# Split float32 products with the high parts first, one low-part buffer, ten row buffers and six 512-column tiles

## The chip, the cores and the metric

The kernel runs on one core of a Trainium2 chip. The metric is the device time of one execution in microseconds: 4555.81 us is the median of three executions before the change (4544.87 to 4565.71). TensorE multiplies into PSUM, VectorE and ScalarE do the elementwise work, GpSimd issues the gathers by index, and SyncE (SP) issues the other transfers. Each engine runs its own queue in order, and an instruction that waits for a semaphore holds back all that stand behind it on that engine.

## The reference, cut to what matters

One step of a hybrid decoder layer on a prompt of 1024 tokens of width 1024 and on eight sample tokens. Three mixers (an SSD state scan, a convolution of width 31, attention over a memory of 256 tokens) are fed from one projection; a gated sum of them goes through an output projection and a norm; then come the experts, and a second norm.

```
proj = x @ w_in
...
x = _layer_norm(ALPHA * x + merged @ w_out, ln1_g, ln1_b)
x = _layer_norm(ALPHA * x + _peer_ffn(x, ...), ln2_g, ln2_b)
```

The experts (PEER) choose, for each token and each of eight heads, 16 of 128 x 128 experts. Each chosen expert is one row of `peer_u` (a dot product with the token, then gelu, then the gate) and one row of `peer_v` (added with that weight):

```
qv = (t @ w_q).reshape(nt, PEER_HEADS, 2, PEER_DHALF)
s = jnp.einsum('thkd,hknd->thkn', qv, sub_keys)
...
act = jax.nn.gelu(jnp.einsum('td,thkd->thk', t, u), approximate=False)
return jnp.einsum('thk,thkd->td', gate * act, v)
```

## The kernel before

The prompt is worked off in three groups of 256, 384 and 384 tokens, features on the partitions. Per group `front` projects and starts the scan, `main` does the mixers and the output projection, `norm1` and `routing` norm and choose the experts.

**Products.** `product` multiplies one 1024 x 128 piece of a weight with the group's tokens, eight matmuls over the contraction. For the input projection and for the experts' first table the operands are split into a high part, rounded to float32r, and a low part, the rest: `load_w` loads `wr` (four buffers), ScalarE copies it to `wh` (L189), VectorE subtracts to `wl` (L191), and `mm3` runs three matmuls for each of the eight pieces of the contraction: high by high, high by low, low by high (L200). The other products run plain float32 from `wr` (L211).

**Gathered experts, groups 0 and 1.** While the next group is in `main`, `spread`, called before every product, sets some row steps of the group before into the queues, by a table of paces; each counts as a late instruction of low priority. `block_u` gathers one row of `peer_u` for each of 128 tokens into a buffer `uv` (GpSimd L442, 512 KB), and VectorE multiplies it with the tokens and sums (L455). `block_v` gathers four rows of `peer_v`, and TensorE adds them up by 32-column strips into `va` (L501). Near the end `block_v2` does that sum on VectorE instead (L544). All these rows share the buffers `uv`, eight of 4 KB a partition (`UVB`).

**Group 2: all experts, densely.** `dense_group` goes through 128 blocks c of 128 experts. `activations` makes the gelu of a product of `peer_ut` with all tokens; `weigh` multiplies with the gates (L1353); `split` makes the high and low part of the result (L176, `b` from `acc`). Then the block of `peer_v` is loaded in two halves into 512-column tiles `e` (`E2B`, seven), split into `vh` and `vl` (L164, L176), and 18 matmuls add into six PSUM tiles (L1385, three token blocks by two halves by three pairs of parts). The first 24 products after the first six are made earlier and read back from `ad`. `wh`/`vh` share a name with two buffers, and so do `wl`/`vl`. The rest of group 1's rows ride along here. The last norm takes its scale and shift rows through buffers of `wl`.

**What sets the order.** The program is scheduled before it runs: instructions are ordered per engine by priority and by when their inputs and buffers are free in the scheduler's own model, and the tiles get their places in that order. So a change of a buffer count can move any instruction. `blk` tiles are 28 general blocks of 392 columns.

Of the kernel before, what the change touches and what calls it, by code (L numbers as in the profile page):

```python
# [9 lines left out]
F32R = mybir.dt.float32r  # L10
# [8 lines left out]
P = 128  # L19
# [5 lines left out]
TB = N // P  # L25
# [4 lines left out]
EPS = 1e-5  # L30
NEG = -3.0e38
TAPS = 31
UVB = 8
TICKS = (4, 6, 5)
PTICK = (1, 1, 0)

# [10 lines left out]
STEP = 4  # L47
VLAG = 6
TLAG = 10
E2B = 7  # L50
BLKB = 28
WRB = 4

C_CW, C_CB, C_D, C_NW = 0, 96, 120, 136
# [9 lines left out]
def f32(ap):  # L64
    return ap.bitcast(F32)
# [3 lines left out]
def hybrid_layer(ctx: ExitStack, tc, I, O):  # L69
    nc = tc.nc  # L70
    pe, act, dve, pool, sp = nc.tensor, nc.scalar, nc.vector, nc.gpsimd, nc.sync
# [3 lines left out]
    accp = ctx.enter_context(tc.tile_pool(name="accp", bufs=8))  # L75
    blkp = ctx.enter_context(tc.tile_pool(name="blkp", bufs=BLKB))
    rawp = ctx.enter_context(tc.tile_pool(name="rawp", bufs=3))
    wp = ctx.enter_context(tc.tile_pool(name="wp", bufs=3))
# [11 lines left out]
    def e2(dt=F32):  # L90
        return ep.tile([P, 512], dt, name="e2", bufs=E2B)

# [88 lines left out]
    def load_raw(src):  # L181
        wr = wp.tile([P, 8, P], F32, name="wr", bufs=WRB)
        sp.dma_start(wr, src)
        return wr

    def load_w(src):
        wr = load_raw(src)
        wh = wp.tile([P, 8, P], F32R, name="wh", bufs=2)
        act.activation(wh, wr, AF.Copy)  # L189
        wl = wp.tile([P, 8, P], F32R, name="wl", bufs=2)  # L190
        dve.tensor_tensor(wl, wr, f32(wh), op=OP.subtract)  # L191
        return wh, wl

    def mm3(ps, w, xh, xl, nk=8, k0=0):
        wh, wl = w
        n = 3 * nk
        i = 0
        for k in range(nk):
            for a, b in ((wh, xh), (wh, xl), (wl, xh)):
                pe.matmul(ps, a[:, k], b[k0 + k], start=(i == 0), stop=(i == n - 1))  # L200
                i += 1

    def product(ps, src, xs):

# [220 lines left out]
    def layer_norm2(r, pn, junk, rows=None):  # L425

        s = rp.tile([P, 4], F32, name="ln2d" if rows else "ln2s", bufs=2)[:pn]
        dve.tensor_reduce(s[:, 0:1], r, axis=AX.X, op=OP.add)
        act.activation(s[:, 1:2], s[:, 0:1], AF.Copy, scale=-1.0 / D)
        act.activation(junk, r, AF.Square, bias=s[:, 1:2], accum_out=s[:, 2:3])  # L430
        act.activation(s[:, 3:4], s[:, 2:3], AF.Ln, scale=1.0 / D, bias=eps[:pn])
        act.activation(s[:, 3:4], s[:, 3:4], AF.Exp, scale=-0.5)
        rpool, rname, rbufs = rows or (pep, "uv", UVB)
        g2 = rpool.tile([P, D], F32, name=rname, bufs=rbufs)
        sp.dma_start(g2, I["ln2"][0:1].to_broadcast([P, D]))
        dve.scalar_tensor_tensor(r, r, s[:, 1:2], g2[:pn], op0=OP.add, op1=OP.mult)
        b2 = rpool.tile([P, D], F32, name=rname, bufs=rbufs)
        sp.dma_start(b2, I["ln2"][1:2].to_broadcast([P, D]))
        dve.scalar_tensor_tensor(r, r, s[:, 3:4], b2[:pn], op0=OP.mult, op1=OP.add)

    def gather(dst, table, idx_col):
        pool.indirect_dma_start(out=dst, out_offset=None, in_=table,  # L442
                                in_offset=bass.IndirectOffsetOnAxis(ap=idx_col, axis=0))
# [3 lines left out]
    def block_u(g, c, idx, gate):  # L447
# [4 lines left out]
        for s in range(P):  # L452
            u = pep.tile([P, D], F32, name="uv", bufs=UVB)
            gather(u, I["peer_u"], idx[:, c, s:s + 1])
# [25 lines left out]
    def block_v(g, c, idx, av, avt, ixt):  # L480
# [23 lines left out]
        for m in range(32):  # L504
            vs = []
            for j in range(4):
                v = pep.tile([P, D], F32, name="uv", bufs=UVB)
                gather(v, I["peer_v"], ixt[:, 32 * j + m:32 * j + m + 1])
# [7 lines left out]
        while not done:  # L516
            yield
        xr = pep.tile([P, D], F32, name="uv", bufs=UVB)
        sp.dma_start(xr, x1d[g][c])
# [3 lines left out]
        active.pop()  # L523
        layer_norm2(xr, P, pep.tile([P, D], F32, name="uv", bufs=UVB))
        sp.dma_start(O[f"yp{g}"][c], xr)

    def block_v2(g, c, idx, av):

        acc = pep.tile([P, D], F32, name="uv", bufs=UVB)
        yield from second_table(P, P, idx[:, c], av, acc)  # L530
# [6 lines left out]
    def second_table(pn, ns, idx, av, acc):  # L537
        for s in range(ns):
            v = pep.tile([P, D], F32, name="uv", bufs=UVB)[:pn]
            gather(v, I["peer_v"], idx[:, s:s + 1])  # L540
            if s == 0:
                dve.tensor_scalar(acc, v, av[:, 0:1], None, op0=OP.mult)
            else:
                dve.scalar_tensor_tensor(acc, v, av[:, s:s + 1], acc, op0=OP.mult, op1=OP.add)  # L544
            yield
# [739 lines left out]
    def dense_group(G):  # L1285
# [50 lines left out]
        while active:  # L1336
            due[:] = 0.0, 8.0
            spread()
        outs = [psp.tile([P, 512], F32, name=nm, bufs=nb)
                for nm, nb in (("mm", 2), ("mm", 2), ("ss", 2), ("ss", 2), ("va", 2), ("va", 2))]  # L1340
# [18 lines left out]
        for c in range(P):  # L1359
            if c + PRE < P:  # L1360
                if c == 2 * EARLY:
                    keep_tokens(G)
                pace[0] = PACE[-2 if c + PRE < early else -1]
                if c + PRE < early:
                    spread()
                    a = accp.tile([P, NW], F32, name="acc")[:, :nt]
                    sp.dma_start(a, ad[:, c + PRE])
                else:
                    a = activations(c + PRE, xs)
                ahead.append(a)  # L1370
                weigh(c + PRE)
            if c + 1 < P:
                ahead[c + 1] = split(ahead[c + 1], nt)
            vh, vl = (wp.tile([P, 1024], F32R, name=n, bufs=2) for n in ("wh", "wl"))
            for dh in range(2):
                hs = slice(dh * 512, dh * 512 + 512)
                v = e2()
                sp.dma_start(v, I["peer_v"][c * P:(c + 1) * P, hs])
                split(v, 512, hl=(vh[:, hs], vl[:, hs]))
            (ah, al), ahead[c] = ahead[c], None  # L1380
            for tbk in range(TB):
                ts = slice(tbk * P, (tbk + 1) * P)
                for i, (a, v) in enumerate(((ah, vh), (ah, vl), (al, vh))):
                    for dh in range(2):
                        pe.matmul(outs[2 * tbk + dh], a[:, ts], v[:, dh * 512:dh * 512 + 512],  # L1385
                                  start=(c == 0 and i == 0), stop=(c == P - 1 and i == 2))
        for tbk in range(TB):
            x1 = wp.tile([P, D], F32, name="wr", bufs=WRB)
            sp.dma_start(x1, x1d[g][tbk])
            for dh in range(2):  # L1390
                hs = slice(dh * 512, dh * 512 + 512)
                dve.scalar_tensor_tensor(x1[:, hs], x1[:, hs], ALPHA, outs[2 * tbk + dh], op0=OP.mult, op1=OP.add)
            junk = wp.tile([P, D], F32, name="wh", bufs=2)
            layer_norm2(x1, P, junk, (wp, "wl", 2))
            sp.dma_start(O[f"yp{g}"][tbk], x1)

    bg.append(memory())
# [120 lines left out]
```

## Time and profile before

| | |
|---|---|
| median of 3 executions | 4555.81 us (4544.87, 4555.81, 4565.71) |
| the profiled execution | 4556.38 us, span 4554.6 us |
| TensorE matmul busy | 3933.1 us (86%), 19901 matmul records |
| weight loads | 3047.6 us (67%), beside the matmuls |
| VectorE | 3289.7 us (72%) |
| ScalarE | 1751.8 us (38%) |
| GpSimd | 1593.4 us (35%) |
| moved by DMA | 1199.42 MB, mean 263 GB/s |
| mean granted TensorE clock | 0.936 |

"Span" is the time from the first to the last instruction of the profiled execution, and all rows are of that execution. "Busy" is time in which an engine works; a wait is the idle time of an engine in front of an instruction, put down to what ended it. Matmuls overlap each other: a product's length is read from the chain of waits, where each piece lasts until the next begins, rather than from the duration of its matmuls. Where the text says 1000 to 1400 us, it is counted from the start of the span: group 0 takes up to about 850, group 1 to about 1950, group 2's mixers to about 2950, then routing and the start of the dense stage to about 3560.

### The profile page before, as it was taken

To read this page: it belongs to the slowest core of one execution; us is meant where nothing else is said; L and a number is where in the kernel's file an instruction comes from. 1 tells how busy PE (TensorE), PEld (TensorE's weight loads), DVE (VectorE), ACT (ScalarE), POOL (GpSimd) and SP (SyncE) were. 2 spreads that over 40 slices of the span, in tenths; PEclk is the share of its full clock that TensorE was granted. 3 is DMA by queue.
4 is the path that set the end of the run, shared out by engine and by line. 5 is a ranking of instruction groups with operands and counts; after the bars stand their busy time and mean duration, and the time that the engine had idled before them with its cause. 6 is when DMAs were issued, how large, how long until landed. Compare 5 with 4: busy or idle time off the path is not lost. (4 is left out here: it accounts for less than half of the span.)

```text
span 4554.6 us, 58299 instructions
## 1 busy us (share of the span) xinstructions
PE 3933.1 (86%) x19901; PEld 3047.6 (67%) x19901; DVE 3289.7 (72%) x7235; ACT 1751.8 (38%) x3696; POOL 1593.4 (35%) x1316
## 2 busy tenths in 40 slices
PE   8998899688898788975888888888996999889996
PEld 8888788567675455553665665445664788778895
DVE  4458835869698546675766796458996899888876
ACT  5475525346432204342362332113562333333333
POOL 0000000123333554413444536534322566556631
PEclk9999999899899998987999999999997999999998
DMA  5435555556677898835878879978879999999985
GB/s 176 149 124 171 180 164 169 202 205 226 220 241 245 302 343 311 291 139 178 282 282 321 304 260 337 341 236 282 305 283 312 359 382 393 343 317 304 389 280 188
DMA packets 410043, 1199.42 MB, mean 263 GB/s; under 512 B 42465, under 2 KB 111713, under 8 KB 407569
## 3 DMA queue, kind: packets, MB, share of 16 engines
q0 software_dynamic: 186880, 679.56, 42.2%
q1 hardware_dynamic: 222864, 516.13, 32.8%
q8 instruction: 157, 2.57, 0.2%
q14 instruction: 142, 1.16, 0.1%
HBM read 1141.59 MB, written 53.93 MB: 262 GB/s over the span
## 5 line engine op out<-in xcount | busy, mean ns | idle before, releaser
L442 POOL DMA_INDIRECT uv<-in_peer_u,idx x640 | 759.0, 1186 | 1831.9 <-DVE idx L422 852.1
L200 PE MATMUL mm<-xt,wh 128*128 128x384 f32 (+1 forms) x4224 | 1045.5, 333 | 37.5 <-ACT b L923 23.9
L455 DVE SCALAR_TENSOR_TENSOR uv<-uv,x 128x1024 f32<-128x1024 f32 x640 | 775.7, 1220 | 395.0 <-DMA uv<-in_peer_u,idx 347.1
L200 PEld LDWEIGHTS mm<-xt,wh 128*128 128x128 f32 x4224 | 745.3, 193 | 100.3 <-issue 33.1
L211 PE MATMUL mm<-b,wr 128*128 128x256 f32 (+2 forms) x2304 | 724.9, 467 | 60.9 <-ACT b L739 34.1
L200 PE MATMUL mm<-xt,wl 128*128 128x384 f32 (+1 forms) x2112 | 692.0, 328 | 37.7 <-DVE wl L191 37.5
L189 ACT ACTIVATE wh<-wr 128x1024 fp32r<-128x1024 f32 x362 | 382.9, 1058 | 864.4 <-PE mm L200 327.0
L442 POOL DMA_INDIRECT uv<-in_peer_v,ixt x384 | 427.6, 1113 | 688.1 <-PE va L501 205.5
L211 PEld LDWEIGHTS mm<-b,wr 128*128 128x128 f32 x2304 | 438.4, 196 | 310.3 <-issue 45.4
L191 DVE TENSOR_TENSOR wl<-wr,wh 128x1024 fp32r<-128x1024 f32 x362 | 441.9, 1221 | 247.1 <-ACT wh L189 229.6
L442 POOL DMA_INDIRECT uv<-in_peer_v,idx x256 | 348.2, 1360 | 345.0 <-DVE uv L544 194.2
L200 PEld LDWEIGHTS mm<-xt,wl 128*128 128x128 f32 x2112 | 406.9, 193 | 57.6 <-DVE wl L191 43.4
L678 DVE SCALAR_TENSOR_TENSOR b<-raw,cc,b 128x384 f32<-128x384 f32 (+1 forms) x720 | 408.7, 569 | 9.9 <-ACT b L676 3.4
L544 DVE SCALAR_TENSOR_TENSOR uv<-uv,av 128x1024 f32<-128x1024 f32 (+1 forms) x269 | 343.5, 1280 | 12.9 <-DMA uv<-in_peer_v,idx 9.9
L501 PE MATMUL va<-uv,slide 128*32 128x512 f32 x1536 | 228.2, 714 | 133.3 <-DMA uv<-in_peer_v,ixt 133.3
L501 PEld LDWEIGHTS va<-uv,slide 128*32 128x32 f32 x1536 | 45.0, 120 | 244.4 <-DMA uv<-in_peer_v,ixt 148.6
L200 PE MATMUL st<-b,wh 128*128 128x384 f32 x784 | 205.7, 344 | 0.5 <-ACT b L832 0.5
L200 PE MATMUL tp<-b,wh 128*128 128x384 f32 x784 | 204.5, 342 | 0.0
L164 ACT ACTIVATE b<-acc 128x384 fp32r<-128x384 f32 x128 | 66.8, 525 | 348.4 <-PE va L1385 261.7
L176 DVE TENSOR_TENSOR wl<-e,wh 128x512 fp32r<-128x512 f32 x256 | 165.1, 684 | 24.2 <-ACT wh L164 22.1
L1385 PE MATMUL mm<-wh,b 128*128 128x512 f32 x512 | 165.2, 404 | 13.7 <-ACT b L164 10.1
L1385 PE MATMUL va<-wh,b 128*128 128x512 f32 x512 | 164.5, 403 | 10.9 <-DVE uv L522 10.9
(409 smaller groups left out, 6382.8 us busy)
## 6 DMA issues: line engine op xcount, KB each, us to landing
wr<-in_win SPq DMA_DIRECT2D x264, 512.0 KB
wr<-in_peer_ut SPq DMA_DIRECT2D x128, 512.0 KB
e<-in_peer_v SPq DMA_DIRECT2D x256, 256.0 KB
wr<-in_wso SPq DMA_DIRECT2D x48, 512.0 KB
wr<-in_wq SPq DMA_DIRECT2D x48, 512.0 KB
gd<-xt SPq DMA_DIRECT2D x16, 1536.0 KB
xt<-gd SPq DMA_DIRECT2D x16, 1536.0 KB
wr<-in_wmo SPq DMA_DIRECT2D x24, 512.0 KB
```

What stands on the lines that cost most here:

```text
L164: act.activation(hi, src, AF.Copy)
L176: dve.tensor_tensor(l, src, f32(h), op=OP.subtract)
L189: act.activation(wh, wr, AF.Copy)
L191: dve.tensor_tensor(wl, wr, f32(wh), op=OP.subtract)
L200: pe.matmul(ps, a[:, k], b[k0 + k], start=(i == 0), stop=(i == n - 1))
L211: pe.matmul(ps, w[:, k], xs[k], start=(k == 0), stop=(k == 7))
L442: pool.indirect_dma_start(out=dst, out_offset=None, in_=table, in_offset=bass.IndirectOffsetOnAxis(ap=idx_col, axis=0))
L455: dve.scalar_tensor_tensor(u, u, 1.0, x1, op0=OP.mult, op1=OP.mult, accum_out=av[:, s:s + 1])
L501: before = pe.matmul(va[dh][32 * j:32 * j + 32], w[:, j, 31 - m:63 - m], vs[j][:, dh * 512:dh * 512 + 512], start=(m == 0), stop=(m == 31) ...
L544: dve.scalar_tensor_tensor(acc, v, av[:, s:s + 1], acc, op0=OP.mult, op1=OP.add)
L678: dve.scalar_tensor_tensor(cv, raw[:, i:i + nt], col(C_FW, j * TAPS + i), cv, op0=OP.mult, op1=OP.add)
L1385: pe.matmul(outs[2 * tbk + dh], a[:, ts], v[:, dh * 512:dh * 512 + 512], start=(c == 0 and i == 0), stop=(c == P - 1 and i == 2))
```

## The change

The matmuls of a split product are the same, in another order: first, for each piece of the contraction, the two that read the high part of the weight, then all that read the low part. For the experts' values the three token blocks first run high by high and low by high, then all run high by low. `wl` and `vl` have one buffer instead of two. `UVB` goes from eight to ten, `E2B` from seven to six, `BLKB` from 28 to 27, and the scale and shift rows of the last norm take buffers of `wr`.

```diff
-UVB = 8
+UVB = 10
...
-E2B = 7
-BLKB = 28
+E2B = 6
+BLKB = 27
...
-        wl = wp.tile([P, 8, P], F32R, name="wl", bufs=2)
+        wl = wp.tile([P, 8, P], F32R, name="wl", bufs=1)
...
-        for k in range(nk):
-            for a, b in ((wh, xh), (wh, xl), (wl, xh)):
-                pe.matmul(ps, a[:, k], b[k0 + k], start=(i == 0), stop=(i == n - 1))
-                i += 1
+        for k, a, b in [(k, wh, x) for k in range(nk) for x in (xh, xl)] + [(k, wl, xh) for k in range(nk)]:
+            pe.matmul(ps, a[:, k], b[k0 + k], start=(i == 0), stop=(i == n - 1))
+            i += 1
...
-            vh, vl = (wp.tile([P, 1024], F32R, name=n, bufs=2) for n in ("wh", "wl"))
+            vh, vl = (wp.tile([P, 1024], F32R, name=n, bufs=nb) for n, nb in (("wh", 2), ("wl", 1)))
...
-            for tbk in range(TB):
+            for tbk, i, a, v in ([(t, i, a, vh) for t in range(TB) for i, a in enumerate((ah, al))]
+                                 + [(t, 2, ah, vl) for t in range(TB)]):
                 ts = slice(tbk * P, (tbk + 1) * P)
-                for i, (a, v) in enumerate(((ah, vh), (ah, vl), (al, vh))):
-                    for dh in range(2):
-                        pe.matmul(outs[2 * tbk + dh], a[:, ts], v[:, dh * 512:dh * 512 + 512],
-                                  start=(c == 0 and i == 0), stop=(c == P - 1 and i == 2))
+                for dh in range(2):
+                    pe.matmul(outs[2 * tbk + dh], a[:, ts], v[:, dh * 512:dh * 512 + 512],
+                              start=(c == 0 and i == 0), stop=(c == P - 1 and i == 2))
...
-            layer_norm2(x1, P, junk, (wp, "wl", 2))
+            layer_norm2(x1, P, junk, (wp, "wr", WRB))
```

The order of the built programs shows what moves. On TensorE in the dense stage, before: the end of a block's activation product (into PSUM tile `tp`, weights `wh`/`wl`) and the first matmuls of the expert values (into `mm` and `ss`, where `wh`/`wl` are the value parts):

```order
L200 MATMUL tp<-b,wh 128x384 x2
L200 MATMUL tp<-b,wl 128x384
L1385 MATMUL mm<-wh,b 128x512 x2
L1385 MATMUL mm<-wl,b 128x512 x2
L1385 MATMUL mm<-wh,b 128x512 x2
L1385 MATMUL ss<-wh,b 128x512 x2
L1385 MATMUL ss<-wl,b 128x512 x2
```

The same block on TensorE after the change, whole:

```order
L199 MATMUL tp<-b,wh 128x384 x16
L199 MATMUL tp<-b,wl 128x384 x8
L1384 MATMUL mm<-wh,b 128x512 x4
L1384 MATMUL ss<-wh,b 128x512 x4
L1384 MATMUL va<-wh,b 128x512 x4
L1384 MATMUL mm<-wl,b 128x512 x2
L1384 MATMUL ss<-wl,b 128x512 x2
L1384 MATMUL va<-wl,b 128x512 x2
```

Both low parts are now read in one run at the end of their group. On VectorE in the dense stage, before, one expert block (`uv` rows of the second table, `wl` from `wr` the weight's low part, `wl` from `e` the two halves of the values, `b` from `acc` the low part of the activations):

```order
L191 TENSOR_TENSOR wl<-wr,wh 128x1024
L1353 TENSOR_TENSOR acc<-acc,xt 128x384
L544 SCALAR_TENSOR_TENSOR uv<-uv,av 128x1024 x2
L176 TENSOR_TENSOR wl<-e_32780,wh 128x512
L176 TENSOR_TENSOR wl<-e_32784,wh 128x512
L176 TENSOR_TENSOR b<-acc,b 128x384
L544 SCALAR_TENSOR_TENSOR uv<-uv,av 128x1024 x2
```

And after:

```order
L191 TENSOR_TENSOR wl<-wr,wh 128x1024
L543 SCALAR_TENSOR_TENSOR uv<-uv,av 128x1024 x2
L176 TENSOR_TENSOR wl<-e_32487,wh 128x512
L1352 TENSOR_TENSOR acc<-acc,xt 128x384
L176 TENSOR_TENSOR wl<-e_32491,wh 128x512
L543 SCALAR_TENSOR_TENSOR uv<-uv,av 128x1024
L176 TENSOR_TENSOR b<-acc,b 128x384
L543 SCALAR_TENSOR_TENSOR uv<-uv,av 128x1024
```

The two rows now follow the weight's low part at once, and the gates' multiplication stands between the halves of the values. On VectorE in a convolution of group 1 (`b` from `raw`: its taps), before:

```order
L191 TENSOR_TENSOR wl<-wr,wh 128x1024
L678 SCALAR_TENSOR_TENSOR b<-raw,cc,b 128x384 x6
L191 TENSOR_TENSOR wl<-wr,wh 128x1024
L678 SCALAR_TENSOR_TENSOR b<-raw,cc,b 128x384 x7
L455 SCALAR_TENSOR_TENSOR uv,av<-uv,x_7972 128x1024
L678 SCALAR_TENSOR_TENSOR b<-raw,cc,b 128x384
```

And after:

```order
L677 SCALAR_TENSOR_TENSOR b<-raw,cc,b 128x384 x14
L191 TENSOR_TENSOR wl<-wr,wh 128x1024
L677 SCALAR_TENSOR_TENSOR b<-raw,cc,b 128x384 x13
L454 SCALAR_TENSOR_TENSOR uv,av<-uv,x_7972 128x1024
L677 SCALAR_TENSOR_TENSOR b<-raw,cc,b 128x384
```

Of the two low parts that stood within the taps one is left; the next one comes after the end of this convolution's taps and its four rows, as the second one's successor did before.

## Rows read from the trace of the kernel before

**Rows 1.** Stretches: window, length, busy PE, PEld, DVE, ACT, POOL; PEclk, DMA share, GB/s.

```profile
1000.00:1400.00 400.00, 360.35 (x1770) 298.37 (x1769) 339.66 (x605) 186.06 (x427) 130.30 (x105) 0.95 0.67 225
1400.00:1950.00 550.00, 465.28 (x2091) 298.42 (x2090) 340.07 (x826) 145.65 (x308) 256.59 (x234) 0.93 0.83 298
...
2090.00:2500.00 410.00, 354.13 (x1777) 242.25 (x1776) 253.22 (x427) 166.19 (x436) 192.11 (x172) 0.92 0.82 289
2500.00:2950.00 450.00, 381.93 (x1703) 259.83 (x1702) 322.04 (x571) 111.27 (x247) 234.36 (x201) 0.96 0.87 315
2950.00:3450.00 500.00, 429.09 (x2054) 263.62 (x2052) 399.46 (x1457) 205.77 (x256) 162.54 (x144) 0.94 0.77 277
3560.00:4220.00 660.00, 609.05 (x2919) 538.90 (x2918) 578.70 (x773) 225.45 (x374) 403.14 (x290) 0.96 1.00 350
4220.00:4510.00 290.00, 285.02 (x1399) 254.53 (x1397) 221.33 (x256) 100.94 (x167) 122.68 (x88) 0.99 0.85 301
```

**Rows 2.** Waits, whole span: who, for whom: us in total, times, longest us.

```profile
POOL uv L442 <- DVE uv L455: 783.2, 262, 38.8
...
POOL uv L442 <- PE va L501: 344.4, 75, 27.2
```

**Rows 3.** Waits in 1400:1950, then in 2090:2950, then in 2950:3450.

```profile
DVE uv L455 <- DMA uv<-in_peer_u,idx: 119.2, 57, 5.9
...
PE va L501 <- DMA uv<-in_peer_v,ixt: 40.7, 15, 4.4
...
DVE uv L455 <- DMA uv<-in_peer_u,idx: 151.7, 79, 5.2
...
PE va L501 <- DMA uv<-in_peer_v,ixt: 67.4, 24, 7.8
...
DVE uv L455 <- DMA uv<-in_peer_u,idx: 29.9, 20, 5.9
...
PE va L501 <- DMA uv<-in_peer_v,ixt: 25.2, 6, 10.8
```

**Rows 4.** Chain of waits, 2800:2950: start us, us, what.

```profile
2821.62 7.68 DMA uv<-in_peer_v,ixt
...
2829.35 3.47 PE va L501 x16
...
2839.11 7.56 DMA uv<-in_peer_v,ixt
```

**Rows 5.** VectorE's groups in 3560:4220: busy us, mean ns, idle before and releasers.

```profile
L544 DVE SCALAR_TENSOR_TENSOR uv<-uv,av 128x1024 f32<-128x1024 f32 (+1 forms) x162 | 206.5, 1279 | 9.6 <-DMA uv<-in_peer_v,idx 8.2 <-DMA uv<-in_peer_v,s_idx 1.3
L455 DVE SCALAR_TENSOR_TENSOR uv<-uv,x 128x1024 f32<-128x1024 f32 x109 | 131.8, 1218 | 31.7 <-DMA uv<-in_peer_u,idx 31.6
L176 DVE TENSOR_TENSOR wl<-e,wh 128x512 fp32r<-128x512 f32 x142 | 91.3, 682 | 2.6 <-ACT b L832 2.0 <-ACT wh L164 0.6
L191 DVE TENSOR_TENSOR wl<-wr,wh 128x1024 fp32r<-128x1024 f32 x67 | 81.6, 1218 | 8.0 <-ACT wh L189 7.9
L176 DVE TENSOR_TENSOR b<-acc,b 128x384 fp32r<-128x384 f32 x76 | 41.9, 552 | 1.4 <-ACT b L832 0.7 <-ACT b L164 0.6
L1353 DVE TENSOR_TENSOR acc<-acc,xt 128x384 f32<-128x384 f32 x68 | 37.8, 556 | 8.5 <-ACT acc L1296 2.7 <-DMA acc<-ad 2.3 <-ACT wh L189 1.8
```

**Rows 6.** Chain of waits, 4300:4340: a product, and a third of the value matmuls.

```profile
4304.37 4.20 PE tp L200 x24
4308.57 1.40 PE mm L1385 x6
```

**Rows 7.** TensorE's waits in 3450:4210.

```profile
PE st L200 <- DVE wl L191: 22.3, 7, 8.2
PE mm L1385 <- DVE wl L176: 19.5, 11, 4.3
PE tp L200 <- DVE wl L191: 14.1, 8, 3.2
```

## Prediction

> **What bounds the kernel now.** I read the stage table first [rows 1]. From 1000 to 3450 us, while groups 1 and 2 run through the layer and the gathered expert rows of the group before ride along, TensorE is busy 85 to 90% of each stretch, VectorE 62 to 85%. TensorE idle is 39.7 us in 1000 to 1400, 84.7 in 1400 to 1950, 55.9 in 2090 to 2500, 68.1 in 2500 to 2950 and 70.9 in 2950 to 3450: each is the length less PE busy. The first is 9.9% of its stretch; the next three are 208.7 us of 1410, 14.8%, and the gathers per microsecond are what grew (105 in 400 us against 607 in 1410, POOL's counts). The granted clock mixes the two levels, 1.2 and 2.4 GHz, and the mean is 0.95 in the first and 0.92 to 0.96 in the others. In the dense stage (3560 to 4220) DVE is busy 88% and the DMA share is 1.00; only from 4220 on is TensorE the bound, at 98%.
>
> Second, who waits for gathers [rows 2, 3]. GpSimd's gathers mostly stand until a buffer is free: 783 us for VectorE's row products (`uv` L455), 344 for TensorE's strips (`va` L501). What a late gather then costs is in [rows 3]: VectorE stands 119.2 + 151.7 + 29.9 = 300.8 us in 156 waits, TensorE 40.7 + 67.4 + 25.2 = 133.3 us in 45. A mean wait is 1.9 us on VectorE and 3.0 on TensorE, the longest 5.9 and 10.8. The chain of waits in the last products of group 2 [rows 4] shows the loop: 7.7 us until the rows of a strip have landed, 3.5 us of strips, and 9.8 us after that landing the next one begins. So up to 3450 us the kernel is a TensorE program disturbed by buffer-starved gathers; after that VectorE, DMA and TensorE are within a few per cent of each other.
>
> **The change part by part.** Nothing is computed more or less: the instructions on TensorE, VectorE, ScalarE and GpSimd are the same in number, and GpSimd's order of gathers is the same. What moves is when buffers come free.
>
> *Ten row buffers.* A gather may start two rows earlier. In 1400 to 1950 GpSimd issues 234 gathers in 550 us, in 2090 to 2950 373 in 860 [rows 1]: one per 2.3 us, so two rows are 4.6 us of lead on the average. Rows also stand in bursts of three or four, and there two rows are 2 x 1.3 = 2.6 us (a 1.22 us product and its accumulator read, [rows 5]). 4.6 us cover the mean wait of either engine whole, 2.6 us cover the mean on VectorE, and neither covers the longest. I take 60% of the waits away; the ends are 30% (landing gets longer as more is in flight) and 100%.
> TensorE: 0.6 x 133.3 = 80 us, of which I count three quarters, 60 us, since VectorE's and ScalarE's results are late in the same places and some of the time only changes its name. VectorE: 0.6 x 300.8 = 180 us of standing. Where VectorE is 62% busy (1400 to 1950, 2090 to 2500) it catches up and little arrives; I take one in seven, 25 us. A check from the other side: were the 208.7 us of idle brought down to the 9.9% of 1000 to 1400, it would be 139.6, so 69 us; the 25.2 us of strip waits after 2950 come on top, 94 in all for a full cure. 85 us is most of that, and I keep it because a shorter idle time also leaves less of the 1.2 GHz level (0.92 and 0.93 against 0.95 [rows 1]).
> In the dense stage VectorE stands 31.6 + 8.2 us for rows [rows 5], on an engine that is the bound there; but the DMA share is 1.00 at 350 GB/s. I take 15 us of the 40.
>
> Here a page of the Trainium skill gives another size. "DMA: Bandwidth & Descriptors" (section "Anatomy of one DMA — SWDGE (gpsimd) path") fits a gather's time as about 2.0 us plus bytes over 436e3 per us; for 524,288 bytes that is an estimate of 3.2 us. The trace shows 7.68 and 7.56 us [rows 4], more than double. By the page 4.6 us of lead would be more than a whole landing and all waits would go, which is the second rival's sum; by the rows part of them stays.
>
> *High parts first, one low-part buffer.* A product of 24 matmuls takes 4.20 us, 18 expert-value matmuls take 3 x 1.40 us [rows 6]. The low part was wanted at the third matmul, now at the seventeenth of 24 (16/24 x 4.20 = 2.8 us later than the start) or the thirteenth of 18 (2.8 us too). Against that, a low part can't be written before the last low matmul of the product before has read its buffer, where before two were in hand. So the subtraction (1.22 us, [rows 5]) has a slot of 2.8 us when products follow each other, and whatever stands behind it in VectorE's queue (rows, hence GpSimd's buffers; taps of a convolution; the subtractions for the values) now waits with it for TensorE. Gain: the waits for low parts are 22.3 + 14.1 + 19.5 = 55.9 us in the dense stage [rows 7], but VectorE is the bound there: per expert block it has 1.22 + 2 x 0.68 + 0.55 + 0.56 + 4 x 1.28 = 8.8 us of work [rows 5] against TensorE's 4.20 + 4.20 = 8.4, so TensorE waits for it in one place or another and I count nothing. Cost: VectorE, the bound, can now be made to wait. In the new order two rows (2.6 us) stand behind the product's subtraction, then the two value subtractions with one multiplication between them (1.9 us), which have to be done inside 2.8 us of high matmuls. That fits with 0.9 us to spare, and a row that lands late by more breaks it. In the convolutions the new order sets 17 taps and four rows between two low parts where it had set 10 and four. I price this from nothing lost to 1 us lost at each of 104 blocks, less the 55.9 us if they are regained: minus 56 to plus 104, and take plus 15, near the low end because the same standing VectorE work fits inside 8.8 us.
>
> *Six 512-column tiles, 27 blocks, LayerNorm rows in `wr`.* The value loads run three expert blocks ahead instead of three and a half, 25 us at 8.4 us a block against landings of some 8 us, so they stay hidden behind TensorE's blocks. The attention and SSD stages have one tile less of slack, and the last norm has to share four buffers between its rows and the stored token. No row prices these; the bounds are 0 and 30 us, and I take 10.
>
> The sum: -60 - 25 - 15 + 15 + 10 = -75 us. The profiled execution took 4556.38 us with a span of 4554.6; the median of three is 4555.81, so the two can be used alike. 4556 - 75 = **4481 us**.
>
> **The rivals.** (a) *DMA sets the pace.* Two more gathers in flight only lengthen every landing. For it: DMA share 0.82 to 0.87 in 2090 to 2950 and 1.00 in the dense stage. Against it: from 2090 to 2950 there are 289 to 315 GB/s beside 350 later [rows 1], and GpSimd waits for buffers, not for transfers [rows 2]. Then only the bursts profit, some 25% of 85 us, and the costs stay: 4556 - 21 + 25 = 4560; with the 30 us of unpriced costs at nothing it is 4556 - 21 + 15 = 4550, which I take.
> (b) *All waits go.* For it: 4.6 us exceeds the mean wait on both engines. The full cure was 94 us, the clock's return from its mean of 0.936 over the 1410 us to 0.95 another 20, half of the dense 40 us 20, less 15 of costs: 4556 - 119 = 4437.
> (c) *Lock-step, slower.* One low buffer ties VectorE to TensorE twice per expert block. It decides when a row's landing is late by more than the 0.9 us of spare time in most blocks; the dense stage has 271 row products [rows 5] on saturated DMA, and a late one delays the value subtraction, that TensorE's low matmuls, those the next subtraction, and no second buffer absorbs it. At 1 us a block that is 104 us, and the convolutions of groups 1 and 2 (16, 3 us each) add 48; with 85 us gained earlier the sum is +67: 4623. At half that price and with half the gather gain, 4556 + 76 - 42 = 4590; I take 4595.
>
> **How the numbers follow.** Chances: my forecast (4445 to 4533) 0.50, (b) 0.13, (a) 0.21, (c) 0.16. A measurement of this kernel can tell about 0.5%, 23 us, from no change. Faster by more: the forecast and (b), 0.63. Within: (a), 0.21. Slower by more: (c), 0.16. The range leaves out the part of (b) below 4425 and half of (c): 4425 to 4590.
>
> **What would show it.** Right: VectorE's waits for `uv` from peer_u up to 3450 us fall from 301 to about 120 us and TensorE's for strips from 133 to about 55; the idle of TensorE between 1400 and 2950 falls below 150 us; the start of the dense stage comes 60 to 90 us earlier, and its length changes by less than 25 us. Low parts: waits of VectorE for TensorE in front of the weights' low subtraction appear, without TensorE waiting longer for low parts than the 56 us of before. Rival (a) shows as row waits that hardly change while GpSimd's waits for buffers shrink; (b) as strip waits under 20 us; (c) as a dense stage that is longer, with TensorE waiting for `wl` in most blocks. I am wrong if the start of the dense stage doesn't move.

## The result, and the profile after

The changed kernel takes 4505.7 us (median of four executions, 4480.56 to 4520.81) beside 4553.36 us for the kernel before on the same chip: a ratio of 0.988, with a 95% interval of 0.985 to 0.990. That is faster by 1.2%, or about 55 us by this ratio (the two medians lie 48 us apart). The forecast was 4481 us, with a range of 4425 to 4590. The profiled execution took 4500.78 us with a span of 4499.0, so its span is 55.6 us shorter.

The stage table of the changed kernel answers to [rows 1] line by line. Its columns are: window, length, busy PE, PEld, DVE, ACT, POOL, then PEclk, DMA share, GB/s.

```profile
1000.00:1400.00 400.00, 359.70 (x1754) 297.00 (x1752) 325.51 (x579) 184.92 (x424) 118.76 (x99) 0.94 0.65 215
1400.00:1950.00 550.00, 484.26 (x2235) 315.84 (x2234) 359.97 (x864) 156.95 (x332) 282.40 (x246) 0.95 0.86 312
...
2090.00:2500.00 410.00, 362.44 (x1824) 250.22 (x1815) 261.95 (x443) 166.43 (x423) 223.01 (x186) 0.92 0.85 307
2500.00:2950.00 450.00, 387.01 (x1692) 262.25 (x1694) 314.31 (x563) 123.15 (x271) 222.59 (x189) 0.94 0.83 301
2950.00:3450.00 500.00, 452.21 (x2164) 288.41 (x2157) 419.10 (x1484) 214.88 (x266) 165.77 (x146) 0.97 0.84 300
3560.00:4220.00 660.00, 612.29 (x2944) 541.77 (x2942) 585.09 (x766) 235.38 (x374) 422.91 (x293) 0.97 1.00 356
```

TensorE's idle time in the three stretches from 1400 to 2950 is now 65.7, 47.6 and 63.0 us, 176.3 in all, where it was 208.7. In 1000 to 1400 it has not moved (40.3 against 39.7).

The waits over the whole span, for VectorE's low parts, for the gathered rows, and GpSimd's for buffers (which engine and line waited for whom: us in total, times, longest):

```profile
POOL uv L441 <- DVE uv L454: 795.9, 247, 73.6
ACT wh L189 <- DMA wr<-in_win: 344.6, 77, 15.3
POOL uv L441 <- PE va L500: 323.5, 72, 26.2
DVE uv L454 <- DMA uv<-in_peer_u,idx: 164.7, 85, 5.9
DVE wl L191 <- PE mm L199: 134.0, 61, 8.0
...
PE va L500 <- DMA uv<-in_peer_v,ixt: 56.3, 20, 5.5
```

Beside [rows 2], GpSimd's waits for a free buffer stand where they were (783 and 344 us before). Its own waits don't tell whether its rows come in time. The waits of the consumers do. By stretch (1400:1950, then 2090:2950, then 2950:3450), as in [rows 3]:

```profile
DVE uv L454 <- DMA uv<-in_peer_u,idx: 55.5, 27, 5.9
...
PE va L500 <- DMA uv<-in_peer_v,ixt: 20.0, 8, 4.0
...
DVE uv L454 <- DMA uv<-in_peer_u,idx: 92.5, 48, 5.0
...
PE va L500 <- DMA uv<-in_peer_v,ixt: 24.6, 8, 5.5
...
PE va L500 <- DMA uv<-in_peer_v,ixt: 11.6, 4, 5.0
...
DVE uv L454 <- DMA uv<-in_peer_u,idx: 1.9, 2, 1.2
```

VectorE's three sums add up to 149.9 us (300.8 before), TensorE's to 56.2 (133.3 before).

Where the time came from is read by putting the same instruction of the two traces side by side, on VectorE's timeline (start, length). The first gate multiplication of the dense stage, before and then after:

```profile
3438.51 2.90 DVE L1353 TENSOR_TENSOR acc<-acc,xt 128x384 f32<-128x384 f32 x6
```

```profile
3384.34 2.90 DVE L1352 TENSOR_TENSOR acc<-acc,xt 128x384 f32<-128x384 f32 x6 [4.62 <-DMA xt<-gd]
```

The dense stage starts 54 us earlier, which is nearly the whole gain. But the way there isn't straight. The same low-part subtraction (the 166th of 362, in group 1), before and then after:

```profile
1465.41 1.22 DVE L191 TENSOR_TENSOR wl<-wr,wh 128x1024 fp32r<-128x1024 f32 x1
```

```profile
1495.31 1.22 DVE L191 TENSOR_TENSOR wl<-wr,wh 128x1024 fp32r<-128x1024 f32 x1
```

The subtraction comes 30 us later, but TensorE doesn't lose that much. It starts the product that reads this low part 12 us later, before and then after:

```profile
1488.88 0.81 PE L200 MATMUL mm<-xt,wh 128*128 128x384 f32 x2
```

```profile
1500.84 3.28 PE L199 MATMUL mm<-xt,wh 128*128 128x384 f32 x16
```

With two buffers VectorE made the low part 23 us ahead of its product; with one it made it 6 us ahead. So group 1 is 12 us behind at this point. That has come back by the end of the group (the output projection's last run of matmuls ends at 1726 us before and 1724 after), and the gain comes behind it. Inside the dense stage the gain grows to 85 us at the 81st block and falls to 62 at the 111th, as these rows show, before and then after:

```profile
4071.62 0.54 DVE L1353 TENSOR_TENSOR acc<-acc,xt 128x384 f32<-128x384 f32 x1
...
4344.21 0.55 DVE L1353 TENSOR_TENSOR acc<-acc,xt 128x384 f32<-128x384 f32 x1
```

```profile
3986.97 0.54 DVE L1352 TENSOR_TENSOR acc<-acc,xt 128x384 f32<-128x384 f32 x1
...
4282.18 0.55 DVE L1352 TENSOR_TENSOR acc<-acc,xt 128x384 f32<-128x384 f32 x1
```

### The profile page after: what moved, and what is told of

Read it like the earlier page. It is cut to its first block, busy times and chain, and to the rows that moved or that the text cites. A ratio compares the mean times of both kernels' runs of the same rounds, so it can differ in the third digit from the quotient of the medians.

```text
span 4499.0 us, 58420 instructions
## 1 busy us (share of the span) xinstructions
PE 3934.4 (87%) x19901; PEld 3054.9 (68%) x19901; DVE 3279.1 (73%) x7235; ACT 1772.8 (39%) x3692; POOL 1630.0 (36%) x1316
## 5 line engine op out<-in xcount | busy, mean ns | idle before, releaser
L454 DVE SCALAR_TENSOR_TENSOR uv<-uv,x 128x1024 f32<-128x1024 f32 x640 | 773.3, 1220 | 182.3 <-DMA uv<-in_peer_u,idx 164.7
L199 PE MATMUL mm<-xt,wh 128*128 128x384 f32 (+1 forms) x4224 | 775.3, 334 | 46.2 <-ACT b L922 28.5
L199 PEld LDWEIGHTS mm<-xt,wh 128*128 128x128 f32 x4224 | 685.5, 192 | 109.4 <-issue 33.2
L189 ACT ACTIVATE wh<-wr 128x1024 fp32r<-128x1024 f32 x362 | 383.2, 1059 | 795.3 <-DMA wr<-in_win 344.6
L441 POOL DMA_INDIRECT uv<-in_peer_v,ixt x384 | 445.9, 1161 | 546.4 <-PE va L500 179.6
L191 DVE TENSOR_TENSOR wl<-wr,wh 128x1024 fp32r<-128x1024 f32 x362 | 442.0, 1221 | 231.5 <-PE mm L199 134.0
L199 PE MATMUL mm<-xt,wl 128*128 128x384 f32 (+1 forms) x2112 | 402.7, 331 | 51.1 <-DVE wl L191 49.1
L199 PEld LDWEIGHTS mm<-xt,wl 128*128 128x128 f32 x2112 | 347.8, 193 | 69.8 <-DVE wl L191 57.3
L164 ACT ACTIVATE wh<-e 128x512 fp32r<-128x512 f32 x256 | 150.1, 626 | 385.7 <-PE va L1384 211.5
L500 PE MATMUL va<-uv,slide 128*32 128x512 f32 x1536 | 215.2, 665 | 63.5 <-DMA uv<-in_peer_v,ixt 56.3
L1384 PE MATMUL mm<-wh,b 128*128 128x512 f32 x512 | 146.4, 403 | 44.7 <-ACT b L164 16.5
L199 PE MATMUL tp<-b,wh 128*128 128x384 f32 x784 | 153.5, 350 | 0.0
L210 PE MATMUL mm<-acc,wr 128*128 128x256 f32 (+2 forms) x512 | 144.6, 441 | 9.4 <-DVE b L812 7.6
L199 PEld LDWEIGHTS tp<-b,wh 128*128 128x128 f32 x784 | 146.9, 199 | 4.7
```

Of the source, the lines that this page charges most:

```text
L164: act.activation(hi, src, AF.Copy)
L210: pe.matmul(ps, w[:, k], xs[k], start=(k == 0), stop=(k == 7))
L454: dve.scalar_tensor_tensor(u, u, 1.0, x1, op0=OP.mult, op1=OP.mult, accum_out=av[:, s:s + 1])
L500: before = pe.matmul(va[dh][32 * j:32 * j + 32], w[:, j, 31 - m:63 - m], vs[j][:, dh * 512:dh * 512 + 512], start=(m == 0), stop=(m == 31) ...
```

## The experiments

A theory for a sum of five terms has to be tested term by term. Theory A is the prediction's: the rows carry the gain, the order by itself gives little, the single low buffer and the small tiles cost little. The rivals B say that another part carries the gain, or that the parts buy the same slack. Each kernel is compared with the kernel before on the same chip; where a ratio is turned into microseconds, it is multiplied with 4553. The ratio isn't that of the two medians, which can differ from it by some 10 us.

**1. The order alone.** The kernel before, with the two new loops over the matmuls; two low parts, eight rows.

```diff
-        for k in range(nk):
-            for a, b in ((wh, xh), (wh, xl), (wl, xh)):
...
+        for k, a, b in [(k, wh, x) for k in range(nk) for x in (xh, xl)] + [(k, wl, xh) for k in range(nk)]:
...
+            for tbk, i, a, v in ([(t, i, a, vh) for t in range(TB) for i, a in enumerate((ah, al))]
+                                 + [(t, 2, ah, vl) for t in range(TB)]):
```

> The kernel before with the new order of matmuls alone: both low parts keep two buffers, rows stay eight. Theory A (the row buffers carry the gain, the order by itself is worth little): 4540 to 4560 us, ratio 0.997 to 1.002; VectorE's waits for rows of peer_u stay near 347 us and TensorE's for strips near 133; TensorE's waits for low parts (about 95 us over the span before) shrink to about 40, hidden by VectorE's own work. Rival B (the order carries the gain, by high parts that are given back a third of a product earlier): about 4500 us, ratio 0.988, with row waits unchanged.

Measured: 4521.82 us, ratio 0.991 (0.989 to 0.994). The order gives 40 us by the ratio (the medians lie 30 apart) without any of the buffers, so A's 4540 to 4560 was wrong; B's 4500 wasn't reached. TensorE's waits for gathered rows and for low parts in this kernel:

```profile
PE va L500 <- DMA uv<-in_peer_v,ixt: 126.9, 45, 10.8
...
PE mm L1384 <- DVE wl L176: 24.7, 10, 5.4
PE mm L199 <- DVE wl L191: 23.8, 4, 22.4
...
PE st L199 <- DVE wl L191: 17.5, 8, 4.7
...
PE tp L199 <- DVE wl L191: 5.2, 2, 4.5
```

The strips wait as before. The low parts add up to 71.2 us, where the same four rows of the kernel before add up to 94.8 (37.5 in the mixers, 23.7, 14.1 and 19.5 in the dense stage). TensorE has 23.6 us less to wait for low parts and is busy 10.0 us less; together these are nearly as large as the 34.1 us by which this profiled span (4520.5) is shorter. But they don't lie where the time is gained. From the start of the 111th product to that of the 181st (1015.5 to 1763.4 us before, 1008.4 to 1717.7 here) this kernel gains 38.6 us, and there TensorE's waits for low parts are only 2.2 us before and 0.8 here. Rival B's mechanism is in the trace too: ScalarE waits less until TensorE gives a high-part buffer back, here for the products into `mm`, before and then in this kernel:

```profile
ACT wh L189 <- PE mm L200: 327.0, 105, 12.5
```

```profile
ACT wh L189 <- PE mm L199: 252.7, 95, 8.3
```

VectorE's waits for ScalarE's high part fall with it, from 229.6 to 182.0 us. No run separates the two, so that the order gains is shown, and by which of them it gains is open.

**2. The single low buffer on top of it, with eight rows.** The changed kernel, with rows and tiles put back.

```diff
-UVB = 10
+UVB = 8
...
-E2B = 6
-BLKB = 27
+E2B = 7
+BLKB = 28
```

> The changed kernel with eight row buffers, seven 512-column tiles and 28 blocks: new order and one low-part buffer are left. Theory A: slower than before by what the single low buffer costs, 10 to 40 us: 4565 to 4595, ratio 1.002 to 1.009; row waits as before (about 350 and 130 us); VectorE waits for TensorE in front of low parts some 100 to 190 us in all. Rival B: about 4500 us, ratio 0.988. If it is at 4553 within 10, the single buffer is free.

Measured: 4605.77 us, ratio 1.011 (1.008 to 1.014). The sign is A's, the size is not: against the order alone, taking away the second low buffer (the norm's rows move with it) costs 1.011 - 0.991 = 2.0%, about 90 us. TensorE's low-part waits are 107.3 us where they were 71.2, VectorE stands 116.6 us for TensorE in front of L191, and the strips still wait 124.4 us.

**3. Nine rows.** The changed kernel with one row buffer less: `UVB = 9`.

> The changed kernel with nine row buffers instead of ten, all else the same. Theory A: between eight and ten, 4530 to 4555 us, ratio 0.995 to 1.000; VectorE's row waits 220 to 280 us, TensorE's strip waits 80 to 105. Rival B (order) and a rival in which small shifts of the schedule carry the gain: about 4500, ratio 0.988, whatever the row waits do.

Measured: 4562.85 us, ratio 1.001 (0.999 to 1.003), as slow as the upper end of A and a little more. VectorE waits 214.7 us for rows (164.7 with ten, 298.8 with eight), TensorE's strips 93.0 us (56.3 and 124.4). The tenth row is worth 0.988 against 1.001, some 60 us; from eight to nine it is 1.0% or 46 us, with the price of the small tiles, which kernel 2 doesn't have, already taken off. Each row takes away a quarter to three tenths of the strips' waits of the kernel with eight.

**4. The small tiles alone.** The kernel before with `E2B = 6` and `BLKB = 27`.

> The kernel before with six 512-column tiles and 27 blocks alone. Theory A: what these two cost, 0 to 15 us: 4550 to 4570, ratio 0.999 to 1.004. A rival in which they cost as much as the rows bring: over 4580, ratio over 1.006; then the changed kernel without them would be far faster.

Measured: 4581.51 us, ratio 1.007 (1.005 to 1.009), so 31 us, where I had taken 10 and drawn the end at 30.

**5. The old order with the changed buffers.** The changed kernel with both loops over the matmuls as before (the diff of experiment 1, reversed).

> The changed kernel with the matmuls of a split product in the old order (low part read at the third matmul and from there on), everything else as changed, the single low-part buffer too. Theory A (the new order is what makes one buffer bearable): each split product ends with a read of the only low part, and the next one wants its low part at its third matmul, some 0.35 us in, while the subtraction takes 1.22 us and starts only then: 0.9 us or more are exposed at most of 384 weight products and at 128 expert-value blocks, so 4506 + 300 to 450 us, ratio 1.05 to 1.09, with TensorE waiting for low parts by that sum. Rival B (the order's gain is the 40 us seen with two buffers, and the scheduler hides the rest): 4540 to 4560, ratio 0.997 to 1.002.

Measured: 4726.02 us, ratio 1.037 (1.034 to 1.040), 220 us slower than the changed kernel. Theory A's direction, but its size was 300 to 450. TensorE's waits:

```profile
PE mm L200 <- DVE wl L191: 112.3, 78, 25.6
PE mm L1385 <- DVE wl L176: 97.5, 83, 7.7
...
PE va L501 <- DMA uv<-in_peer_v,ixt: 29.6, 11, 7.1
```

Low parts now hold TensorE for 210.3 us in all (77.9 in the changed kernel). The strips wait only 29.6 us, in a kernel that is 220 us slower; that a TensorE which stands elsewhere gives the rows time to land would explain it. So a shorter wait for rows is not yet a gain. Instead of 0.9 us at most of the products and blocks there are the 78 waits and 83 waits of the two rows above, with a mean of 1.4 and 1.2 us.

**6. The order of the values alone.** The kernel before, with only the loop over the expert values in the new order.

> The kernel before with the new order in the expert values alone (products in the old order, all buffers as before). Theory A (the gain of the order came in the products: with both orders it was there before any expert values run, 44 us at 1716, and the dense stage gave 16 us back): 0.998 to 1.004. Rival B (the values' order gains too, by the 20 us that TensorE waits for their low parts): 0.994 to 0.997.

Measured: 4569.32 us, ratio 1.003 (1.001 to 1.006): no gain, 15 us of loss if anything. So what the order gained in experiment 1 it most likely gained in the products. That fits experiment 1, where the dense stage starts 50 us earlier than in the kernel before and ends only 34 us earlier.

**7. Three raw-weight buffers.** The price of 4 KB, to be spent in the next versions: the changed kernel with `WRB = 3`.

> The changed kernel with three buffers for raw weights instead of four, and nothing else: the price of the 4 KB that the next versions spend. Theory A (a weight of 512 KB is wanted every 4 us or more and three are enough): ratio to the kernel before 0.985 to 0.994, as the changed kernel's 0.988. Rival B (the loads' landing beside the gathers' traffic needs the fourth): 1.00 to 1.02, with new waits of ScalarE for the raw weight.

Measured: 4510.9 us, ratio 0.991 (0.988 to 0.994). It can't be told apart from the changed kernel. ScalarE waits 389.4 us for raw weights of the input projection instead of 344.6, but TensorE's waits for ScalarE's high parts only go from 19.2 to 21.2.

**8. Two low buffers again.** Kernel 7 with the 4 KB spent on the second low buffer: new order, two low parts, ten rows, small tiles.

```diff
-WRB = 4
+WRB = 3
...
-        wl = wp.tile([P, 8, P], F32R, name="wl", bufs=1)
+        wl = wp.tile([P, 8, P], F32R, name="wl", bufs=2)
...
-            vh, vl = (wp.tile([P, 1024], F32R, name=n, bufs=nb) for n, nb in (("wh", 2), ("wl", 1)))
+            vh, vl = (wp.tile([P, 1024], F32R, name=n, bufs=nb) for n, nb in (("wh", 2), ("wl", 2)))
```

> The changed kernel with two low-part buffers again, paid for by three raw-weight buffers: new order, ten rows, small tiles, two low parts. Theory A (the terms add: order -40 us, ninth and tenth row -46 and -60 as found with one low buffer, small tiles +31, the single buffer's +91 gone, from 4552): about 4437, ratio 0.970 to 0.980. Rival B (a second low buffer and two more rows buy the same slack of VectorE, so that with two low parts the rows bring little): 4490 to 4530, ratio 0.986 to 0.995.

Measured: 4469.04 us, ratio 0.981 (0.979 to 0.983): faster than the kernel before and the changed one, and 1.0% faster than kernel 7. It is between the two theories. The second low buffer, worth 90 us with eight rows and full tiles, is worth 47 with ten rows and small tiles. TensorE's waits for rows and low parts:

```profile
PE va L500 <- DMA uv<-in_peer_v,ixt: 74.1, 24, 10.1
...
PE mm L199 <- DVE wl L191: 23.1, 4, 21.2
...
PE st L199 <- DVE wl L191: 16.1, 4, 7.8
...
PE tp L199 <- DVE wl L191: 6.5, 2, 5.7
PE mm L1384 <- DVE wl L176: 4.9, 2, 4.7
```

The low parts are down to 50.6 us from kernel 7's 83.1, and VectorE's wait for TensorE in front of L191 from 105.2 to 17.9.

**9. Full tiles.** Kernel 7 with the 4 KB spent on `E2B = 7` and `BLKB = 28`.

> The changed kernel with seven 512-column tiles and 28 blocks again, paid for by three raw-weight buffers: one low part, ten rows. Theory A (the 31 us that the small tiles cost in the kernel before come back): about 4475, ratio 0.979 to 0.987. Rival B (the small tiles' price came from the old arrangement alone, or a third raw-weight buffer eats it): 4500 to 4520, ratio 0.988 to 0.993.

Measured: 4495.2 us, ratio 0.986 (0.984 to 0.988), 25 us faster than kernel 7. The two intervals lie end to end, so its size is loose, but it agrees with the 31 us of experiment 4.

**10. Two low buffers, nine rows, full tiles.** Kernel 1 with `UVB = 9` and `WRB = 3`.

> The kernel before with the new order of matmuls, nine row buffers and three raw-weight buffers: two low parts, seven 512-column tiles, 28 blocks. Theory A (the terms add: the new order alone gave 4522 us, the third raw-weight buffer costs some 10, the ninth row gives the 46 found with one low buffer): about 4486, ratio 0.982 to 0.988. Rival B (with two low parts a row is worth at most half of that, since the second low buffer already lets VectorE run ahead): 4510 to 4525, ratio 0.989 to 0.994.

Measured: 4505.46 us, ratio 0.990 (0.986 to 0.994). Rival B: beside the order alone (0.991) the ninth row, less what the fourth raw-weight buffer may be worth, gives nothing that can be measured (the two intervals leave some 22 us either way), while with one low buffer it gave 46 us and paid for the small tiles besides. Against kernel 8 it lacks one row and has full tiles, and is 0.9% slower, so there the tenth row is worth some 40 us and the price of the tiles besides. A row's worth has no single value.

**11. Two raw-weight buffers.** Two low parts, ten rows, full tiles, `WRB = 2`.

> New order, two low parts, ten rows, seven 512-column tiles and 28 blocks, paid for by two raw-weight buffers. Theory A (a raw-weight buffer goes on costing some 5 to 15 us each, and the tiles give back the 24 us between the version with full tiles and the one with three raw buffers): 4450 to 4470, ratio 0.977 to 0.982. Rival B (with two buffers a weight's load starts only when the one two products before has been subtracted, and its landing no longer fits under the products): 4520 to 4650, ratio 0.993 to 1.02, with ScalarE's waits for raw weights at well over the 364 us of the version with three.

Measured: 4667.0 us, ratio 1.024 (1.019 to 1.028). Rival B. TensorE's new waits, and ScalarE's behind them:

```profile
PE mm L199 <- ACT wh L189: 57.0, 32, 7.5
PE tp L199 <- ACT wh L189: 49.6, 6, 15.8
```

```profile
ACT wh L189 <- DMA wr<-in_win: 538.1, 134, 14.8
...
ACT wh L189 <- DMA wr<-in_peer_ut: 145.7, 17, 21.2
```

Giving up the fourth raw-weight buffer cost nothing that could be measured (7); giving up the third as well costs some 4% beside kernel 8, which has three and small tiles. Here the high part itself is late, and the new order puts off the low part alone.

**12. Kernel 8 with the values in the old order.** The loop over the expert values as before, all else as in kernel 8.

> The fastest version so far (new order, two low parts, ten rows, small tiles, three raw-weight buffers: 4469 us) with the expert values in the old order of matmuls; the weight products keep the new one. Theory A (the values' new order costs the 15 us that it cost alone in the kernel before): about 4454, ratio 0.974 to 0.979. Rival B (that price belonged to the arrangement of the kernel before; with ten rows and the low parts in time the values' order is indifferent or useful): 4465 to 4485, ratio 0.980 to 0.985.

Measured: 4461.62 us, ratio 0.980 (0.977 to 0.982). It can't be told from kernel 8 (0.979 to 0.983), so whether the values' order costs anything there stays open. Both beat the changed kernel, whose interval begins at 0.985.

The accounts of TensorE in the profiled executions put these side by side (us; idle is span less busy, low parts the sum of TensorE's waits for `wl`):

| kernel | span | busy | idle | waits for strips | for low parts |
|---|---|---|---|---|---|
| before | 4554.6 | 3933.1 | 621.5 | 133.3 | 94.8 |
| order alone (1) | 4520.5 | 3923.1 | 597.4 | 126.9 | 71.2 |
| + one low buffer (2) | 4625.3 | 3970.5 | 654.8 | 124.4 | 107.3 |
| nine rows (3) | 4574.2 | 3948.6 | 625.6 | 93.0 | 87.2 |
| after | 4499.0 | 3934.4 | 564.6 | 56.3 | 77.9 |
| two low buffers (8) | 4453.9 | 3894.4 | 559.5 | 74.1 | 50.6 |

Before and after, busy is the same to 1.3 us, and the 56.9 us of idle time are the gain. Two cautions belong to the other rows. The profiled executions of kernels 2 and 3 are 21 and 13 us above the median of their kernel, that of kernel 8 is 13 below. And kernel 8 gains in another column: beside kernel 7 (span 4501.6, busy 3929.6) it has only 12.5 us less idle time, but 35.2 us less busy time, at mean granted clocks of 0.941 and 0.938. So the fall of the low parts' waits is not most of what its second low buffer is worth there, and why the busy time is shorter is open.

## Why the prediction was right, and where its steps were off

The sign, the mechanism (gathers come earlier, TensorE stands less for strips, the dense stage starts earlier at the same length) and the range were right. The total of -75 us came out at -55. That it came so close is luck in part: errors of much more than 20 us cancelled. By the ratios, taken one after the other: order -40, single low buffer +91, small tiles +31, rows from eight to ten -137 (from 1.011 to 0.988 with the tiles' 31 us in between). The chain is one path among several; experiments 8 and 10 show that along another the terms have other sizes. Since every buffer count also re-orders the program, a term of 15 to 30 us may belong to an arrangement and not to the buffer; no run here separates that.

*Ten row buffers: -100 predicted, -137 along that path.* The waits did what was written: TensorE's strips from 133.3 to 56.2 us up to 3450 (55 predicted), VectorE's row waits from 300.8 to 149.9 (120 predicted). What failed is the share of the strips' time that reaches the end. I counted three quarters and expected TensorE's idle between 1400 and 2950 below 150 us; it is 176.3. The strips lost 63.5 us of waiting there, the idle only 32.4, so half. Nor does the reason hold that I took from the clock for keeping 85 us: with less idle time the mean granted clock rose from 0.93 to 0.95 in 1400 to 1950, but it fell from 0.96 to 0.94 in 2500 to 2950. Over the whole span, while the strips' waits fell by 77.0 us, TensorE's waits for ScalarE's and VectorE's other results (`b`, and the high parts) rose by 41. That is "some of the time only changes its name", with a bigger share than I gave it. Yet the rows were worth more than 100 us in experiments 2 to 4, because with one low buffer a VectorE that stands for a row also delays the subtraction, and TensorE then waits twice for one late row. I had not put that coupling into the rows' term; that it is the reason is argued from experiments 3 and 10 (a ninth row is worth 46 us and the tiles' price with one low buffer, nothing measurable with two), not shown by a row.

*Order and low buffer: +15 predicted, +51 measured, and this is the term that failed most.* It was two terms of opposite sign, and I looked for both in the dense stage. For the dense stage the reading held: it did not get longer (1116.1 us from its first gate multiplication to the end before, 1114.7 after), and the values' order alone gained nothing. TensorE's waits for low parts in 3450 to 4210, the rows that answer to [rows 7]:

```profile
PE mm L1384 <- DVE wl L176: 23.5, 14, 3.9
PE st L199 <- DVE wl L191: 3.0, 2, 2.2
PE tp L199 <- DVE wl L191: 2.3, 2, 1.5
```

28.8 us instead of 55.9. But the order's 40 us and most of the buffer's price lie earlier, in the groups: the first gate multiplication comes at 3388.2 us with the order alone, 50 us earlier than before, and at 3482.0 with one low buffer on top of it (2), 94 us later again. The sum counted nothing for the order and looked for the buffer's price at the dense blocks, and [rows 7] shows the dense stage alone. The whole-span list held a part of it: 37.5 us of TensorE's waits for L191 in the input projection, 23.8 with the order alone, 49.1 after the change. The rest is not in the waits for low parts (experiment 1), and its cause stays open. VectorE's side of the same trade is one row of the page each, before and then after (busy, mean ns, idle before it and what ended most of it):

```profile
L191 DVE TENSOR_TENSOR wl<-wr,wh 128x1024 fp32r<-128x1024 f32 x362 | 441.9, 1221 | 247.1 <-ACT wh L189 229.6
```

```profile
L191 DVE TENSOR_TENSOR wl<-wr,wh 128x1024 fp32r<-128x1024 f32 x362 | 442.0, 1221 | 231.5 <-PE mm L199 134.0
```

VectorE stands about as long in front of the subtraction as before; it used to wait for ScalarE's high part and now waits for TensorE to be done with the only low buffer. The bounds of -56 to +104 that I gave did hold +51.

*Small tiles: +10 predicted, +31 and +25 measured.* I said the value loads stay hidden behind three blocks. ScalarE's waits for them rose from 13.1 to 88.4 us after the change, and with full tiles (9) they are 49.9. But with the small tiles alone (4) they are only 18.7, so the 31 us there are not mainly waits for value loads. That kernel is 23 us late at the end of group 1's output projection, 14 at the start of the dense stage (3452.5 against 3438.5) and 21 at the end of the span, so more of its price lies before the dense stage than in it; in which stage is open.

*The start of the dense stage* came 54 us earlier, just short of the 60 to 90 that I gave.

*The rivals.* (a), DMA sets the pace, fell for groups 1 and 2: the four sums of the consumers' waits for rows between 1400 and 2950 fell by 39 to 64%. But between the 81st and the 111th block of the dense stage, where 23 of 85 us were given back, it may describe what is seen. The chain of waits of the changed kernel in that place shows these rows (start, us, what; an `s_idx` gather fetches 64 rows, half as many bytes as an `idx` gather):

```profile
4082.77 15.54 DMA uv<-in_peer_v,s_idx
4099.96 16.62 DMA uv<-in_peer_v,idx
4118.23 20.80 DMA uv<-in_peer_v,idx
```

In the kernel before the three longest on the chain, at about the same blocks, are:

```profile
4143.47 10.04 DMA uv<-in_peer_v,s_idx
4172.10 10.15 DMA uv<-in_peer_v,idx
4186.68 12.20 DMA uv<-in_peer_v,s_idx
```

And kernel 1, which has eight buffers, has this one there:

```profile
4088.53 16.71 DMA uv<-in_peer_v,idx
```

So a piece of 16.7 us doesn't need ten buffers, and that two more gathers in flight make each of them land later isn't shown. VectorE also has more row work between these two blocks, 153.8 us where it was 141.3 (instructions on `uv`), which by itself could be half of the 23 us.

(b), all waits go, fell with 56 us of strips and 165 of rows left. The Trainium skill's page "DMA: Bandwidth & Descriptors" (section "Anatomy of one DMA — SWDGE (gpsimd) path") led to the same rival; its fit is per DMA, and the landings of 7.68 and 7.56 us [rows 4] don't agree with it, so the measurement decides. The chain shows those gathers that were waited for, so they need not be typical. (c), lock-step, was not what came, but it was the right fear: the kernel of experiment 2, with eight rows, is 50 us slower than the kernel before, and the price of its single low buffer, 90 us, is near the 76 that (c) put on it at half price. But (c) looked for it in the dense stage, and most of it came before (94 of the 105 us between the two profiled spans). That the two rows kept it from deciding, by taking VectorE's lateness away, is argued from experiments 2 to 4.

## What to carry to other kernels

When an operand is split into a high part that is ready early and a low part that a second engine still has to make, run all matmuls on the high part first: that alone gave 0.9% here, and with a single low buffer the old order is 5% slower. It paid in the weight products; for the expert values by themselves no gain was measured. Don't then spend the gain on taking away the second buffer before asking which buffer is truly idle: the fourth raw-weight buffer was worth nothing measurable, and giving that one up instead gave the two fastest versions (ratios 0.981 and 0.980). Price a bundle of buffer counts by runs of its parts, since their worths don't add: going from eight rows to ten, the small tiles included, gave 106 us beside one low buffer (2 and the changed kernel) and 48 beside two (1 and 8, which has one raw-weight buffer less).

## What the runs showed of the hardware

- On the chain of waits, gathers of 512 KB took 7.6 us in group 2 [rows 4]. In the dense stage they took 10.15 us in the kernel before and 16.62 and 20.80 us after the change, at a DMA share of 1.00 and 350 and 356 GB/s; but 16.71 us also in kernel 1, with eight buffers, at 0.97 and 341 GB/s. All of these are gathers that an engine had to wait for.
- TensorE's busy time for the same 19901 matmul records is not fixed: it was 3894.4 us in kernel 8 and 3970.5 in kernel 2, at mean granted clocks of 0.941 and 0.929. The clocks differ by 1.3%, the busy times by 2.0%, so the clock can be a part of it and not all. The old order (5) had 3992.5 us busy at 0.944; why stays open.
